# Retention of a chunk in three blocks between the seven products of an m-gate pair

## The chip, the core and the metric

The kernel runs as one program on one NeuronCore of a Trainium2 chip. The metric is the device time of one execution in microseconds (us). The kernel before was timed three times: 1814.88, 1816.7 and 1818.19 us, median 1816.7 us. A further execution was profiled; it took 1813.31 us, and its profile is the one read below.

## What is computed

The reference is one layer of a hybrid model on 1024 tokens of width 1024: a gated causal convolution and a retention (a linear attention with decay) whose outputs are gated and mixed, then a mixture of 32 experts, a per-layer embedding and a final norm. What the change touches is the retention and the sigmoid gates m_c and m_r:

```python
u, c_g, b_g, q, k, v, sg, m_c, m_r = jnp.split(h @ w_in[i], splits, axis=-1)
...
def step(state, inp):                 # a chunk of 128 tokens, 8 heads
    qb, kb, vb = inp
    scores = jnp.einsum('bhid,bhjd->bhij', qb, kb) * decay_mask
    inner = jnp.einsum('bhij,bhjv->bhiv', scores, vb)
    cross = jnp.einsum('bhid,bhdv->bhiv', qb, state) * q_decay[None, :, :, None]
    state = state * chunk_decay[None, :, None, None] + jnp.einsum(
        'bhjd,bhjv->bhdv', kb * k_decay[None, :, :, None], vb)
    return state, inner + cross
...
o = rmsnorm(o, g_ret[i].reshape(RET_HEADS, RET_DV)).reshape(b_, s_len, V_W)
y_ret = (jax.nn.silu(sg) * o) @ w_out_ret[i]
mixed = jax.nn.sigmoid(m_c) * y_conv + jax.nn.sigmoid(m_r) * y_ret
```

## The kernel before

The program is one long stretch for five engines. TensorE (PE) multiplies, VectorE (DVE) and ScalarE (ACT) move results out of PSUM and prepare operands, GpSimd (POOL) takes powers, and SyncE (SP) issues the DMAs. A scheduler turns the Python code into one fixed list of instructions for each engine; each engine then works through its list in order and waits at an instruction until its operands are ready. So where the scheduler puts an instruction decides what stands behind it when it waits.

Full-precision products are made from three passes: each operand is split into a rounded part and a remainder (`split`, L187: ACT writes the rounded part at L188, DVE the remainder at L189), and `mm3` (L192) multiplies high by high (L193), high by low (L194) and low by high (L195). All these matmuls have 512 columns.

The columns of `w_in` other than q, k and v are multiplied two blocks of 128 columns at a time, a *pair*, by `seven` (L390), which makes the four quarter products of a pair from seven products of half size instead of eight. Each of the seven is 12 matmuls (4 steps of k by 3 passes), into one of four PSUM accumulators called sa, sb, sc and sd. In the order of the code they are S2 into sb, S1 into sd, A11 into sa, S3 into sc, A12 into sa, S4 into sd and A22 into sc. Between A11 and S4 the sums u2 and u3 are formed (L417 on ACT; L418, L421 and L422 on DVE): L421 must have read sc before A22 writes into it, and L422 must have read sd before S4 does. The pieces of the weight (`pc`, six buffers for seven pieces of a pair) are prepared a pair ahead: L408 to L410 form three differences from the raw weight, which a DMA (L391) brings into one buffer, `both[:, 0]`.

The retention runs beside the eight m-gate pairs (L781 to L784): for pair n, `retention(n, ...)` puts chunk n into the program, then `gate_pair` the pair, then `turn()` the transposes that bring the chunk's output into columns. A chunk consists of eight transposes of q and k (L304, `qkp`), the scores (L314, `sp`; eight matmuls, which the trace shows as 16), the outputs (L325 and L329, `op`, in two halves of four heads), the product for the state (L359, `kv`) and the eight transposes of the output (L346, `otp`). In between DVE scales and masks (L306, L316), takes sums of squares (L337), normalises (L339) and updates the state (L364, L365), and ACT copies (L308, L333, L335, L349). No order between the chunk's matmuls and the pair's is written in the code; the scheduler mixes them.

After the m-gate pairs come twelve pairs for the convolution (`conv_pair`), four for `sg` (`sg_pair`), the mixing and output projections, the router, the experts and the end. They have no part in the change.

## Time and profile before

| | |
|---|---|
| three timed runs | 1814.88, 1816.7, 1818.19 us (median 1816.7) |
| the profiled execution | 1813.31 us, span 1811.5 us |
| PE busy | 1734.7 us, 96% of the span |
| DVE / ACT / POOL busy | 1267.3 / 901.3 / 161.2 us (70 / 50 / 9%) |
| chain that ended last | PE 42%, issue 4%, DMA 1%, DVE 1% |
| the m-gate pairs, first product to first conv product | 208.07 to 447.68 us |

The span is the time from the first to the last instruction in the profile. Busy times are those of the hardware profiler; PE's instructions overlap, so that a matmul of 0.39 us may start 0.23 us after the one before, and the useful number is the distance between two starts. "Idle before" is the time in which an engine had nothing running before an instruction, and the name behind the arrow is what the instruction waited for. The page's own costliest groups are the experts' weight splits and matmuls; the stage of the change is about 240 us of the span, and is read from the timeline.

### The profile page before, as it was taken

How to read it: one execution, taken by the hardware profiler on the slowest of the kernel's cores; microseconds unless marked ns; L12 is line 12 of the kernel's file. 1: busy time of each engine (PE TensorE's matmuls, PEld its weight loads, DVE VectorE, ACT ScalarE, POOL GpSimd, SP SyncE). 2: the span in 40 equal slices, each digit the busy share in tenths (PEclk: the TensorE clock that was granted, in tenths of full speed). 3: DMA queues.
4: the chain of work that ended last, by engine and by line, in shares of the span. 5: the costliest groups of instructions: out<-in, count | busy, mean ns of one | idle time of the engine just before them, and what ended most of it. 6: DMA issues, size and time to landing. Idle time of an engine off the chain costs nothing. (4 is left out here: it accounts for less than half of the span.)

```text
span 1811.5 us, 22815 instructions
## 1 busy us (share of the span) xinstructions
PE 1734.7 (96%) x8447; PEld 1347.0 (74%) x8447; DVE 1267.3 (70%) x1747; ACT 901.3 (50%) x1354; POOL 161.2 (9%) x157
## 2 busy tenths in 40 slices
PE   6999999999999999999999998999999999999697
PEld 5878777777778788778988986666666666666486
DVE  5559565655667776656454457999999988888674
ACT  4243343334222223434322336888888877777542
POOL 1000000000000000000000003212122221100010
PEclk9999999999999999999999989999999999999899
DMA  6534433333122216476665969999999999997561
GB/s 227 157 103 136 146 128 115 122 119 109 55 93 94 70 47 200 153 232 206 193 183 162 300 194 358 361 360 379 382 366 379 365 377 353 364 400 282 198 247 67
DMA packets 174629, 397.68 MB, mean 220 GB/s; under 512 B 14796, under 2 KB 101908, under 8 KB 148916
## 3 DMA queue, kind: packets, MB, share of 16 engines
q1 hardware_dynamic: 165012, 378.19, 60.2%
q0 software_dynamic: 9504, 18.02, 3.2%
q8 instruction: 67, 1.10, 0.3%
q14 instruction: 46, 0.38, 0.1%
HBM read 344.77 MB, written 57.68 MB: 222 GB/s over the span
## 5 line engine op out<-in xcount | busy, mean ns | idle before, releaser
L872 DVE TENSOR_TENSOR hc<-raw,hc 128x1024 fp32r<-128x1024 f32 x128 | 154.3, 1223 | 20.7 <-ACT hc L870 18.8
L872 DVE TENSOR_TENSOR hb<-raw,hb 128x1024 fp32r<-128x1024 f32 x128 | 153.8, 1219 | 15.2 <-ACT hb L870 14.3
L872 DVE TENSOR_TENSOR ha<-raw,ha 128x1024 fp32r<-128x1024 f32 x128 | 154.0, 1221 | 13.7 <-ACT ha L870 11.7
L870 ACT ACTIVATE ha<-raw 128x1024 fp32r<-128x1024 f32 x128 | 132.8, 1059 | 26.7 <-PE y L195 15.3
L870 ACT ACTIVATE hb<-raw 128x1024 fp32r<-128x1024 f32 x128 | 132.8, 1057 | 21.2 <-PE u L195 11.9
L870 ACT ACTIVATE hc<-raw 128x1024 fp32r<-128x1024 f32 x128 | 132.6, 1057 | 15.8 <-PE y L195 4.8
L188 ACT ACTIVATE pc<-both 128x512 fp32r<-128x512 f32 x120 | 73.0, 626 | 94.2 <-PE sd L195 31.1
L189 DVE TENSOR_TENSOR pc<-both,pc 128x512 fp32r<-128x512 f32 x120 | 81.2, 687 | 51.3 <-ACT pc L188 50.9
L188 ACT ACTIVATE pc<-bt 128x512 fp32r<-128x512 f32 x48 | 30.0, 625 | 153.0 <-DVE bt L410 137.2
L193 PE MATMUL y<-ph,wys 128*128 128x512 f32 x256 | 100.7, 394 | 4.9 <-ACT wys L188 4.9
L195 PE MATMUL y<-ph,wys 128*128 128x512 f32 x256 | 100.6, 393 | 1.2 <-DVE wys L189 1.2
L194 PE MATMUL y<-pl,wys 128*128 128x512 f32 x256 | 100.2, 391 | 0.0
L193 PE MATMUL sd<-sh,pc 128*128 128x512 f32 x192 | 77.0, 401 | 8.2 <-DVE u L422 8.0
L188 ACT ACTIVATE wys<-wyr 128x1024 fp32r<-128x1024 f32 x32 | 34.0, 1061 | 99.0 <-PE y L195 71.1
L195 PE MATMUL sd<-sh,pc 128*128 128x512 f32 x192 | 76.2, 397 | 0.0
L194 PE MATMUL sd<-sl,pc 128*128 128x512 f32 x192 | 75.4, 392 | 0.0
L189 DVE TENSOR_TENSOR wqs<-wqr,wqs 128x1024 fp32r<-128x1024 f32 x32 | 39.2, 1224 | 49.5 <-ACT wqs L188 49.5
L188 ACT ACTIVATE wqs<-wqr 128x1024 fp32r<-128x1024 f32 x32 | 33.9, 1059 | 70.3 <-PE qa L195 62.4
L718 POOL DMA_INDIRECT xgb<-h2d,ii x32 | 35.5, 1110 | 301.6 <-DVE hd L908 198.3
L193 PEld LDWEIGHTS y<-ph,wys 128*128 128x128 f32 x256 | 48.4, 189 | 15.4 <-ACT wys L188 5.7
L195 PEld LDWEIGHTS y<-ph,wys 128*128 128x128 f32 x256 | 48.5, 189 | 12.2 <-DVE wys L189 2.2
L506 DVE TENSOR_TENSOR msg<-y,msg 128x512 f32<-128x512 f32 x32 | 22.0, 689 | 50.2 <-PE y L195 50.1
(393 smaller groups left out, 4974.8 us busy)
## 6 DMA issues: line engine op xcount, KB each, us to landing
raw<-in_w_exp_gate_dram SPq DMA_DIRECT2D x64, 1024.0 KB, 19.7
raw<-in_w_exp_up_dram SPq DMA_DIRECT2D x64, 1024.0 KB, 19.7
raw<-in_w_exp_down_dram SPq DMA_DIRECT2D x63, 1024.0 KB, 21.8
both<-in_w_in_dram SPq DMA_DIRECT2D x24, 1024.0 KB, 5.8
wqr<-in_w_in_dram SPq DMA_DIRECT2D x32, 512.0 KB, 3.8
qd<-r SPq DMA_DIRECT2D x32, 256.0 KB, 3.1
both<-qd SPq DMA_DIRECT2D x8, 1024.0 KB, 4.8
wyr<-in_w_out_conv_dram SPq DMA_DIRECT2D x16, 512.0 KB, 4.5
```

The source lines that it names most:

```text
L188: a = A.activation(hi, src, AF.Copy)
L189: V.tensor_tensor(lo, src, hi, op=OP.subtract)
L193: T.matmul(o, lh, rh, start=start, stop=False, skip_group_check=skip)
L194: T.matmul(o, lh, rl, start=False, stop=False, skip_group_check=skip)
L195: T.matmul(o, ll, rh, start=False, stop=stop, skip_group_check=skip)
L506: V.tensor_tensor(sg, y, sg, op=OP.mult)
L718: g = P.indirect_dma_start(out=xgs[e % 3], out_offset=None, in_=h2d, in_offset=bass.IndirectOffsetOnAxis(ap=ii[:, 0, e:e + 1], axis=0), bo ...
L870: A.activation(hl[:, 0, q:q + 1024], raw[:, q:q + 1024], AF.Copy)
L872: V.tensor_tensor(hl[:, 1, q:q + 1024], raw[:, q:q + 1024], hl[:, 0, q:q + 1024], op=OP.subtract)
```

## The change

The chunk's work is cut into four functions that `retention` returns, and `seven` calls them at fixed places: `turned` after S2 (the transposes of q and k, and the transposes of the output of the chunk *before*, which are now made by `turn(n - 1)`), `scores` after S1, `outputs` after A11 (both halves of the outputs, and the state product), and `close` (normalising and the update of the state, DVE alone) behind the sum that writes u3. `tc.issue_after(x)` makes the scheduler put what follows behind x on x's engine; it adds no wait. With it the seven products and the three blocks stand on PE in the order of the code. The output of chunk 7 is turned after the last pair by `turn(7)`. The PSUM banks of the blocks are shared out anew (two banks for the transposes of q and k, two for the scores and two for the outputs, where each had one). No operation is added or left out.

```diff
     def mm3(o, lh, ll, rh, rl, start, stop, skip=False):
         T.matmul(o, lh, rh, start=start, stop=False, skip_group_check=skip)
         T.matmul(o, lh, rl, start=False, stop=False, skip_group_check=skip)
-        T.matmul(o, ll, rh, start=False, stop=stop, skip_group_check=skip)
+        return T.matmul(o, ll, rh, start=False, stop=stop, skip_group_check=skip).ins
...
+    osb = [t.rearrange("p (a b) -> p a b", a=4) for t in osbs]
+
+    def bank(name, tag):
+        return ps.tile([128, 4, 128], F32, name=name, tag=tag, bufs=1)
+
+    def turn(n):
+        t0 = n * 128
+        for b in range(2):
+            pt = bank("otp", ("o", "kv")[b])
+            for j in range(4):
+                pe = T.transpose(pt[:, j], osb[b][:, j], ident).ins
+            ot = w2k("ot").rearrange("p (a b) -> p a b", a=4)
+            for j in range(4):
+                A.activation(ot[:, j], pt[:, j], AF.Copy, scale=gret[:, 4 * b + j:4 * b + j + 1])
+            Y.dma_start(out=od[b * 512:(b + 1) * 512, t0:t0 + 128].rearrange("(a p) t -> p a t", p=128), in_=ot)
+        return pe
+
+
     def retention(n, ck):
         first, last = n == 0, n == 7
         Y.dma_start(out=ck, in_=qd[n * 128:(n + 1) * 128])
         q, k, v = ck[:, 0:512], ck[:, 512:1024], ck[:, 1024:2048]
...
+        qt, kt = (w2k(n_).rearrange("p (a b) -> p a b", a=4) for n_ in ("qt", "kt"))
+        sm, rss, kvs = [], [], []
+
+        def turned(pe):
+            for src, dst_, tag in ((q, qt, "tr"), (k, kt, "S")):
+                pt = bank("qkp", tag)
+                for a_ in range(4):
+                    pe = T.transpose(pt[:, a_], src[:, a_ * 128:(a_ + 1) * 128], ident).ins
+                if src is q:
+                    V.tensor_tensor(dst_, pt, qdT, op=OP.mult)
+                else:
+                    A.activation(dst_, pt, AF.Copy)
+            if not first:
+                with tc.issue_after(pe):
+                    pe = turn(n - 1)
+            return pe
+
+        def scores(pe):
+            for par in range(2):
+                sp = bank("sp", ("tr", "S")[par])
+                r = slice(par * 64, par * 64 + 64)
+                with tc.issue_after(pe):
+                    for a_ in range(4):
+                        pe = T.matmul(sp[:, a_], kt[r, a_], qt[r, a_], start=True, stop=True).ins
+                sb = w2k("sb").rearrange("p (a b) -> p a b", a=4)
+                V.tensor_tensor(sb, sp, caus[:, None, :].to_broadcast([128, 4, 128]), op=OP.mult)
+                sm.append(sb)
+            return pe
+
+        def outputs(pe):
             for b in range(2):
+                op = bank("op", ("o", "tr")[b])
+                m_ = 0
+                with tc.issue_after(pe):
+                    for a_ in (2 * b, 2 * b + 1):
+                        for par in range(2):
+                            h = 2 * a_ + par
+                            pe = T.matmul(op[:, h - 4 * b], sm[par][:, a_], v[:, h * 128:(h + 1) * 128],
+                                          start=m_ == 0, stop=first, skip_group_check=True).ins
+                            m_ += 1
+                        if not first:
+                            pe = T.matmul(op[:, (a_ % 2) * 2:(a_ % 2) * 2 + 2], qt[:, a_],
+                                          state[:, a_].rearrange("p (u v) -> p u v", u=2), start=False, stop=True,
+                                          skip_group_check=True).ins
+                A.activation(osb[b], op, AF.Copy)
+                sq = w2k("osq").rearrange("p (a b) -> p a b", a=4)
+                A.activation(sq, op, AF.Square)
+                ss = wk.tile([128, 8], F32, name="oss", tag="sm", bufs=4)
+                V.tensor_reduce(ss[:, 0:4], sq, axis=AX.X, op=OP.add)
+                rss.append(rstd(ss[:, 0:4], DV, "ors"))
+            if last:
+                return pe
+            kvs.append(bank("kv", "kv"))
+            with tc.issue_after(pe):
+                for a_ in range(4):
+                    for par in range(2):
+                        h = 2 * a_ + par
+                        pe = T.matmul(kvs[0][par * 64:par * 64 + 64, a_], k[:, h * 64:h * 64 + 64],
+                                      v[:, h * 128:(h + 1) * 128], start=True, stop=True, skip_group_check=True).ins
+            return pe
+
+        def close():
+            for b in range(2):
+                V.tensor_tensor(osb[b], osb[b], rss[b][:, :, None].to_broadcast([128, 4, 128]), op=OP.mult)
+            for par in range(0 if last else 2):
+                r = slice(par * 64, par * 64 + 64)
+                sv = state[r, :, par * 128:par * 128 + 128]
+                V.tensor_tensor(sv, sv, kvs[0][r], op=OP.add)
+                V.tensor_tensor(sv, sv, Gd[r, :, None].to_broadcast([64, 4, 128]), op=OP.mult)
+
+        return [turned, scores, outputs, close]
...
-    def seven(c0, raw, left, take):
+    def seven(c0, raw, left, take, mid=None):
         Y.dma_start(out=raw.rearrange("p (k n) -> p k n", k=8),
                     in_=w_in[:, c0:c0 + 256].rearrange("(k p) n -> p k n", p=128))
         b = raw.rearrange("p (q k s n) -> p q k s n", q=2, k=4, s=2)
...
             split(src, pc[:, 0], pc[:, 1])
             return pc
 
+
+        pe = []
+
+        def behind():
+            return tc.issue_after(pe[-1]) if mid and pe else nullcontext()
+
         def prod(o, i, pc, first):
             h, l, k0 = left[i]
-            for k in range(4):
-                mm3(o, pc[:, 0, k], pc[:, 1, k], h[k0 + k], l[k0 + k], first and k == 0, k == 3, True)
+            with behind():
+                for k in range(4):
+                    end = mm3(o, pc[:, 0, k], pc[:, 1, k], h[k0 + k], l[k0 + k], first and k == 0, k == 3, True)
+            pe.append(end)
+
+        def step(i):
+            if mid:
+                with behind():
+                    pe.append(mid[i](pe[-1]))
 
         V.tensor_tensor(t3, b22, b12, op=OP.subtract)
         V.tensor_tensor(b12, b12, b11, op=OP.subtract)
         V.tensor_tensor(t2, b22, b12, op=OP.subtract)
         a, b_, c, d = (acc(n) for n in ("sa", "sb", "sc", "sd"))
         prod(b_, 'S2', piece(t2), True)
+        step(0)
         prod(d, 'S1', piece(b12), True)
+        step(1)
         prod(a, 'A11', piece(b11), True)
         u2, u3, c21 = w2k("u2"), w2k("u3"), w2k("c21")
         with tc.high_priority():
             A.activation(u2, a, AF.Copy)
             V.tensor_tensor(u2, b_, u2, op=OP.add)
+        step(2)
         prod(c, 'S3', piece(t3), True)
         with tc.high_priority():
             V.tensor_tensor(u3, c, u2, op=OP.add)
-            V.tensor_tensor(u3, d, u3, op=OP.add)
+            summed = V.tensor_tensor(u3, d, u3, op=OP.add).ins
+        if mid:
+            with tc.issue_after(summed):
+                mid[3]()
...
-    def gate_pair(m, j, raw, left):
+    def gate_pair(m, j, raw, left, mid):
...
-        seven(6144 + m * 1024 + j * 256, raw(), left, take)
+        seven(6144 + m * 1024 + j * 256, raw(), left, take, mid)
...
-        turn = retention(n, both[:, 1])
-        gate_pair(n // 4, n % 4, raw, left)
-        turn()
+        gate_pair(n // 4, n % 4, raw, left, retention(n, both[:, 1]))
+    turn(7)
```

How the instructions stand now is shown at three places of a middle pair (the pairs 1 to 6 read alike). The first is PE's list from S1 on. Here `sb`, `sd` are the accumulators of S2 and S1, `sh`, `sl` the operand's two parts, `qkp` and `otp` the transposes. Before:

```order
L193 MATMUL sd<-sh,pc 128x512
L194 MATMUL sd<-sl,pc 128x512
L304 MATMUL qkp<-cs,both 128x128 x4
L195 MATMUL sd<-sh,pc 128x512
L193 MATMUL sd<-sh,pc 128x512
L194 MATMUL sd<-sl,pc 128x512
L195 MATMUL sd<-sh,pc 128x512
L193 MATMUL sd<-sh,pc 128x512
L194 MATMUL sd<-sl,pc 128x512
L304 MATMUL qkp<-cs,both 128x128 x4
```

And now:

```order
L194 MATMUL sb<-sl,pc 128x512
L195 MATMUL sb<-sh,pc 128x512
L323 MATMUL qkp<-cs,both 128x128 x8
L304 MATMUL otp<-cs,xgb 128x128 x8
L193 MATMUL sd<-sh,pc 128x512
L194 MATMUL sd<-sl,pc 128x512
```

The transposes of q and k, and those of the output, which stood in four runs of four, stand in one run of sixteen between two whole products.

The second place is PE's list from the end of A12 into sa to the start of S4 into sd. Before:

```order
L194 MATMUL sa<-hb,pc 128x512
L195 MATMUL sa<-hb,pc 128x512
L193 MATMUL sc<-hb,pc 128x512
L194 MATMUL sc<-hb,pc 128x512
L195 MATMUL sc<-hb,pc 128x512
L193 MATMUL sc<-hb,pc 128x512
L193 MATMUL sd<-sh,pc 128x512
L194 MATMUL sd<-sl,pc 128x512
```

And now:

```order
L194 MATMUL sa<-hb,pc 128x512
L195 MATMUL sa<-hb,pc 128x512
L193 MATMUL sd<-sh,pc 128x512
L194 MATMUL sd<-sl,pc 128x512
L195 MATMUL sd<-sh,pc 128x512
```

Four matmuls of A22 into sc stood ahead of S4; now S4 follows A12 directly, and A22 comes after it.

The third place is DVE's list from the masking of the scores (`sb<-sp`) to the sum that S4 waits for (the second of the two into the newer `u`, from `sd`). `xgb` holds the outputs that are normalised, `shared` the state, `oss` and `ors` the sums of squares and their roots. Before:

```order
L316 TENSOR_TENSOR sb<-sp,xgb 128x512
L408 TENSOR_TENSOR bt<-both 128x512
L316 TENSOR_TENSOR sb<-sp,xgb 128x512
L409 TENSOR_TENSOR both<-both 128x4x128
L410 TENSOR_TENSOR bt<-both 128x512
...
L365 TENSOR_TENSOR shared<-shared,xgb 64x4x128
L421 TENSOR_TENSOR u_2146<-sc,u_2145 128x512
L339 TENSOR_TENSOR xgb<-xgb,ors 128x512
L422 TENSOR_TENSOR u_2146<-sd,u_2146 128x512
```

And now:

```order
L341 TENSOR_TENSOR sb<-sp,xgb 128x512 x2
L441 TENSOR_TENSOR bt<-both 128x512
L442 TENSOR_TENSOR both<-both 128x4x128
L443 TENSOR_TENSOR bt<-both 128x512
...
L457 TENSOR_TENSOR u_2101<-sc,u_2100 128x512
L189 TENSOR_TENSOR pc<-both,pc 128x512
L458 TENSOR_TENSOR u_2101<-sd,u_2101 128x512
L379 TENSOR_TENSOR xgb<-xgb,ors 128x512 x2
L383 TENSOR_TENSOR shared<-shared,kv 64x4x128 x2
```

Both masks now stand ahead of the first use of the next raw weight, and the normalising and the state's update stand behind both sums; between the sums stands the remainder of one weight piece.

## Rows read from the trace of the kernel before

**Rows 1.** Windows: us from A to B, busy time of each engine, granted clock, DMA.

```profile
208.07:237.24 29.17, 27.38 (x145) 20.96 (x145) 21.22 (x37) 12.47 (x22) 2.70 (x2) 1.00 0.27 92
237.24:267.65 30.41, 29.44 (x158) 22.68 (x156) 17.63 (x30) 11.66 (x26) 2.31 (x2) 1.00 0.36 122
...
389.73:418.97 29.24, 28.29 (x143) 21.82 (x141) 16.50 (x28) 10.47 (x24) 2.32 (x2) 1.00 0.38 126
418.97:447.68 28.71, 28.28 (x143) 21.91 (x142) 15.22 (x28) 11.69 (x25) 2.01 (x2) 1.00 0.30 92
```

**Rows 2.** Waits from 237.2 to 419 us: us in total, times, longest.

```profile
DVE bt L408 <- DMA both<-in_w_in_dram: 11.2, 6, 2.4
...
PE sc L193 <- DVE u L421: 3.3, 6, 0.6
PE sd L193 <- DVE u L422: 2.4, 6, 0.4
```

**Rows 3.** Timeline of PE, pair 4: start, duration, line, operation [idle before].

```profile
330.36 0.66 PE L346 MATMUL otp<-cs,xgb 128*128 128x128 f32 x4
330.77 0.48 PE L195 MATMUL sb<-sh,pc 128*128 128x512 f32 x1
331.09 0.40 PE L193 MATMUL sb<-sh,pc 128*128 128x512 f32 x1
...
335.67 1.15 PE L314 MATMUL sp<-qt,kt 64*128 64x128 f32 x8
336.75 0.50 PE L193 MATMUL sa<-ha,pc 128*128 128x512 f32 x1
...
341.25 0.49 PE L325 MATMUL op<-both,sb 128*128 128x128 f32 x2 [0.40 <-DVE sb L316]
...
344.29 0.71 PE L325 MATMUL op<-both,sb 128*128 128x128 f32 x4
...
345.96 0.58 PE L194 MATMUL sc<-sl,pc 128*128 128x512 f32 x1
346.38 0.39 PE L195 MATMUL sc<-sh,pc 128*128 128x512 f32 x1
...
350.65 0.39 PE L195 MATMUL sa<-hb,pc 128*128 128x512 f32 x1
351.56 0.50 PE L193 MATMUL sc<-hb,pc 128*128 128x512 f32 x1 [0.53 <-DVE u L421]
351.90 0.40 PE L194 MATMUL sc<-hb,pc 128*128 128x512 f32 x1
...
352.36 0.40 PE L193 MATMUL sc<-hb,pc 128*128 128x512 f32 x1
353.16 0.50 PE L193 MATMUL sd<-sh,pc 128*128 128x512 f32 x1 [0.40 <-DVE u L422]
```

**Rows 4.** Timeline of PE at the end of the kernel: a run of eight transposes.

```profile
1734.76 1.04 PE L1135 MATMUL fpt<-cs,yb 128*128 128x128 f32 x8
1735.55 0.48 PE L193 MATMUL fo<-fh,fth 128*128 128x512 f32 x1
```

**Rows 5.** Timeline of PE at the start of pair 0.

```profile
211.50 0.50 PE L195 MATMUL sb<-sh,pc 128*128 128x512 f32 x1 [0.90 <-DVE pc L189]
```

**Rows 6.** Timeline of PE in the first conv pair.

```profile
463.60 0.50 PE L193 MATMUL sd<-sh,pc 128*128 128x512 f32 x1 [1.05 <-DVE u L422]
```

**Rows 7.** Timeline of all engines: one weight piece split after a product's end.

```profile
445.13 0.63 ACT L188 ACTIVATE pc<-both 128x512 fp32r<-128x512 f32 x1 [2.22 <-PE sd L195]
...
445.80 0.69 DVE L189 TENSOR_TENSOR pc<-both,pc 128x512 fp32r<-128x512 f32 x1 [2.58 <-ACT pc L188]
```

**Rows 8.** Timeline of SP: the issue of the raw weight's load in pair 1.

```profile
242.29 0.37 SPq L391 DMA_DIRECT2D both<-in_w_in_dram  x1
```

**Rows 9.** View of the tile `both`: its 33 loads, from issue to landing.

```profile
DMA to landing us min/median/max: 4.7/5.7/8.2
```

**Rows 10.** Timeline of PE, earlier in the kernel: a long wait.

```profile
112.62 0.63 PE L239 MATMUL xtq<-cs,xi 128*128 128x128 f32 x4 [3.44 <-issue]
```

**Rows 11.** Windows, as Rows 1: the stretch that follows that wait.

```profile
114.00:117.40 3.40, 3.40 (x8) 2.40 (x9) 2.67 (x6) 1.62 (x3) 0.55 (x1) 0.50 0.56 144
```

## The prediction

> **What bounds the kernel now.** I read the windows first, then the waits, then PE's timeline. The windows of the m-gate pairs [rows 1] show PE busy 27 to 29 of 29 to 30 us, DVE some 18 to 21, ACT 10 to 12 and the DMA engines at a third; so PE sets the length of this stage, and a microsecond that PE saves here comes off the end. The pairs 1 to 6 run from 237.24 to 418.97 us, 181.7 us or 30.29 each. The waits [rows 2] name what stops PE in them: in each of the six it waits twice for DVE's sums (L421, L422). PE's timeline of one pair [rows 3] shows the same two holes, and something the waits do not list: every time PE goes from the pair's matmuls to a few of the chunk's and back, it loses a tenth or two. The starts of two matmuls of 512 columns are 0.23 us apart (351.90 to 352.36, two steps); behind a run of transposes the next step is 0.32 (330.77 to 331.09), behind outputs 0.42 (345.96 to 346.38).

> **The change, part by part.** No operation is added or removed, so the 84 matmuls of a pair and the chunk's own work stay (scores 1.08 us a half, 335.67 to 336.75; outputs 1.67 a half, 344.29 to 345.96); what can change is waits and passages between them.

> *The two holes before A22 and S4.* From 350.65 to 351.56 PE needs 0.91 where 0.23 is normal, from 352.36 to 353.16 0.80; the first step behind each is 0.34 instead of 0.23 (351.56 to 351.90) [rows 3]. That is 0.68 + 0.57 + 2 x 0.11 = 1.47 us a pair. They arise because A22 starts right behind A12's end and L421 is late in DVE's list, behind the normalising and the state's update. In the new list S4 comes first, A22 last, and DVE has only one weight remainder (L189) between the sums L457 and L458. Does S4 still wait? Counted from the end of S3: L457, L189, L458 are 3 x 0.69 = 2.07 us, and ACT's half of L189 (0.63) runs beside L457 [rows 7]; A12 gives 12 x 0.23 = 2.76 us of cover. Some 0.5 us remain after the hand-overs between engines. I take the 1.47 as gone. If that cover fails, S4 waits by what is missing, and with it the whole rest of PE's list; behind L189 on DVE stand only L458 and what the next pair needs.

> *The mask behind the load.* DVE's first use of the raw weight (L408) waits for its load, 11.2 us in six pairs [rows 2], and the second mask stood behind it; PE waits 0.40 for the mask at 341.25 [rows 3]. Both masks now stand ahead. I take 0.2 as the mean of the six pairs (half of this one).

> *The transposes.* Four runs of four cost 0.41 + 0.09 each (330.36 to 330.77, and the step behind) [rows 3], 2.0 us. A run of eight takes 0.79 [rows 4], so four more cost 0.38; sixteen take 0.79 + 2 x 0.38 + 0.09 = 1.64. Saved 0.36. No row shows sixteen in a run, nor two kinds in one; I take 0.36, between nothing and twice that; a loss would need PE to wait within the run, for banks whose last readers are a block or more back. They need the chunk's load, which can start when the block of outputs has read the chunk before, three products (8.3 us) and S2 (2.8) ahead, and takes 8.2 at most [rows 9]; and outputs that the pair before has normalised.

> *Scores, outputs, state.* Before, they stand in four runs, the state product in a fifth together with transposes; now in two. Two passages less, at 0.09 to 0.19, and their entries: 0.3, between 0 and 0.6.

> *What is moved on the other engines.* ACT's eight copies of the turned outputs come a block earlier than the scores' masks need ACT, beside S1. SP issues the raw weight's load ahead of the two writes of the output instead of behind them; the write's time costs nothing, since nothing reads it before `sg_pair`. The powers on POOL have S3 to run beside. `close` puts four state operations and two normalisings, 6 x 0.69 = 4.1 us of DVE at the duration of rows 7, behind L458, ahead of the pieces t3 and b21 of the next pair, which are needed a whole pair later.

> A middle pair gains 1.47 + 0.2 + 0.36 + 0.3 = 2.33 us, six of them 14.0. Pair 0: PE is idle 29.17 - 27.38 = 1.79 us there [rows 1], 0.90 of it at 211.50 [rows 5], where DVE updates the state before it makes the first remainders. That update now comes later; a wait of 0.3 for the first remainder stays. Half an output's transposes (0.5) leave this pair, and the outputs merge (0.3): 0.6 + 0.9 + 0.5 + 0.3 = 2.3. Pair 7: idle 0.43, and 0.36 + 0.3 from the merging; with `turn(7)` whole behind it, the half turn in the first conv pair goes. But that conv pair's S4 waits 1.05 us for a sum behind a load [rows 6], and what PE reaches earlier there it partly waits: I subtract 0.4. Together 0.7. The sum is 14.0 + 2.3 + 0.7 = 17.0 us. The profiled execution took 1813.3 us (span 1811.5), so it would take 1796.3. The median of the timed runs is 3.4 us above the profiled one, and from it the same sum gives 1799.7 us, which I round to 1800.

> [...]

> **The rivals.** (1) *S4 waits in place of A22.* In a fixed order nothing fills a wait. For it: DVE's remainder between the two sums hangs on ACT, and the cover is only 0.5 us. Against it: DVE has little else there. With the wait of the conv pair, 1.05 us, in seven pairs, the gain is 17.0 - 7.4 = 9.6: 1807. (2) *The passages are free elsewhere*: the merged runs save nothing and only the waits go. Then 6 x 1.67 + 1.5 = 11.5, less 0.4: 1806; if they save twice my value, 6 x 3.0 + 3 = 21: 1796. [...] (4) *The raw weight's load comes too late: slower than before.* A new pair is about 28.0 us, S3 ends three products (8.3) before its end, at 19.7. Between the landing and L457 DVE has eight operations, L441 to L443, L453, two remainders and two sums of squares, 5.5 us at 0.69. So from a landing at 14.2 + 0.5 = 14.7 us on S4 waits, and from 17.0 on the whole 2.33 us are lost. The load is issued about 5 us into the pair (242.29 - 237.24) [rows 8] and takes 5.7, at most 8.2 [rows 9]: it lands at 10.7 to 13.3. The two output writes, now right behind it, speak for longer; that they ran beside it before, too, speaks against it. It would need 12 us; at 13 it lands at 18.0 and costs 3.3 in each of seven pairs, 23.1 against the 17.0: 1823. (5) *No change*: some fixed thing behind the stage, as that load in the first conv pair, gives all back; nothing shows one so long: the wait there is 1.05. That the change doesn't do what it says is excluded by the order.

> **How the numbers follow.** Chances: forecast 0.72 (own range 1795 to 1805), rivals 1 and 2 together 0.16, rival 3 0.03, rival 5 0.05, rival 4 0.04. The bounds of the merging and of the mask give 1794 at the best; to hold 8 in 10 the range reaches to rivals 1 and 2 and a little beyond: 1794 to 1809. About 0.2% (3.6 us) can be told from no change: faster are the forecast and rivals 1 to 3, 0.91; same rival 5, 0.05; slower rival 4, 0.04.

> **What would show it.** In the changed profile: pairs of about 28 us between the first products; no PE wait for L457 or L458; a step of 1.55 us from the first of sixteen transposes to S1; no PE wait for the masks; the raw weight landing 10 to 13 us after the pair's start; granted clock 1.00. Wrong would be: PE idle ahead of S4 or of the blocks in every pair, pairs over 29 us, or the clock at 0.50 in the stage.

## The result, and the profile after

The changed kernel takes 1789.5 us (median of 4 runs, 1787.9 to 1791.6), the kernel before 1816.0 beside it (1814.9 to 1818.2): a ratio of 0.9856, 95% interval 0.9842 to 0.9869. Between the two profiled executions (1813.3 and 1788.2 us) lie 25.2 us. The forecast was 1800, its range 1794 to 1809, from a gain of 17.0. The time lies 4.5 us below the range: the forecast was right in sign and place, and too small in size.

The windows of pairs 0, 1, 6 and 7 after the change (us from A to B, then the busy time of PE, PEld, DVE, ACT and POOL, the granted clock, DMA):

```profile
208.26:233.89 25.63, 25.63 (x142) 20.79 (x142) 19.95 (x34) 11.26 (x19) 2.33 (x2) 1.00 0.31 104
233.89:261.40 27.51, 27.51 (x158) 22.99 (x156) 18.11 (x30) 11.91 (x25) 2.01 (x2) 1.00 0.42 134
371.45:398.96 27.51, 27.51 (x157) 22.99 (x156) 18.04 (x29) 11.91 (x25) 2.01 (x2) 1.00 0.41 134
398.96:426.02 27.06, 27.06 (x149) 22.96 (x148) 16.08 (x27) 12.43 (x26) 2.01 (x2) 1.00 0.32 97
```

Against [rows 1], PE is never idle from pair 1 on: busy time and length are the same number. Pairs 1 to 6 take 27.51 us each, in place of 30.29. The waits of that stretch (us in total, times, longest) hold no row of PE any more; [rows 2] had two. What DVE waits for is now PE and, less, the load:

```profile
DVE u L457 <- PE sc L195: 12.0, 6, 2.0
...
DVE bt L441 <- DMA both<-in_w_in_dram: 6.7, 6, 1.3
```

PE's timeline of pair 5 (start, duration, line, operation), the counterpart of [rows 3]:

```profile
346.66 1.03 PE L323 MATMUL qkp<-cs,both 128*128 128x128 f32 x8
347.53 1.04 PE L304 MATMUL otp<-cs,xgb 128*128 128x128 f32 x8
348.32 0.48 PE L193 MATMUL sd<-sh,pc 128*128 128x512 f32 x1
...
351.25 1.71 PE L339 MATMUL sp<-qt,kt 64*128 64x128 f32 x16
352.89 0.50 PE L193 MATMUL sa<-ha,pc 128*128 128x512 f32 x1
353.22 0.39 PE L194 MATMUL sa<-ha,pc 128*128 128x512 f32 x1
...
358.84 0.60 PE L357 MATMUL op<-shared,qt 128*128 128x256 f32 x2
359.37 1.09 PE L373 MATMUL kv<-both 128*64 128x128 f32 x16
360.39 0.50 PE L193 MATMUL sc<-sh,pc 128*128 128x512 f32 x1
...
366.01 0.39 PE L193 MATMUL sd<-sh,pc 128*128 128x512 f32 x1
```

The transposes take 1.66 us (346.66 to 348.32), forecast 1.55; with the longer step behind them (0.32 in place of 0.23) 1.75, forecast 1.64. The surprise is the scores: both halves in 1.64 us (351.25 to 352.89), where one alone took 1.08 in [rows 3]. And S4 at 366.01 has no wait; DVE's timeline of the same pair says by how much:

```profile
363.49 0.69 DVE L457 TENSOR_TENSOR u<-sc,u 128x512 f32<-128x512 f32 x1 [2.00 <-PE sc L195]
364.15 0.69 DVE L189 TENSOR_TENSOR pc<-both,pc 128x512 fp32r<-128x512 f32 x1
364.76 0.68 DVE L458 TENSOR_TENSOR u<-sd,u 128x512 f32<-128x512 f32 x1
365.37 1.28 DVE L379 TENSOR_TENSOR xgb<-xgb,ors 128x512 f32<-128x512 f32 x2
```

The second sum ends at 365.44, 0.57 us ahead of S4; the normalising follows at once. Where the 25.2 us come from, by starts of first products: pairs 1 to 6 give 16.7 (6 x 2.78), pair 0 3.5 (29.17 to 25.63), pair 7 1.65 (28.71 to 27.06), the first conv pair 0.64 (21.49 to 20.85). That is 22.5. The other 2.7 lie outside: 2.9 behind the first conv pair, less 0.2 by which the stage starts later (208.26 in place of 208.07). In that conv pair PE still waits ahead of S4, 0.4 us longer than in [rows 6], as forecast:

```profile
441.30 0.50 PE L193 MATMUL sd<-sh,pc 128*128 128x512 f32 x1 [1.42 <-DVE u L458]
```

### The profile page after: what moved, and what is told of

Its sections match the earlier page's. It is cut to its first block, busy times and chain, and to the rows that moved or that the text cites. A ratio compares the mean times of both kernels' runs of the same rounds, so it can differ in the third digit from the quotient of the medians.

```text
span 1786.4 us, 22831 instructions
## 1 busy us (share of the span) xinstructions
PE 1720.2 (96%) x8447; PEld 1348.9 (76%) x8447; DVE 1269.6 (71%) x1747; ACT 903.3 (51%) x1354; POOL 157.6 (9%) x157
## 5 line engine op out<-in xcount | busy, mean ns | idle before, releaser
L910 DVE TENSOR_TENSOR hb<-raw,hb 128x1024 fp32r<-128x1024 f32 x128 | 153.9, 1220 | 15.2 <-ACT hb L908 13.8
L189 DVE TENSOR_TENSOR pc<-both,pc 128x512 fp32r<-128x512 f32 x120 | 81.2, 688 | 16.5 <-ACT pc L188 16.2
L189 DVE TENSOR_TENSOR wqs<-wqr,wqs 128x1024 fp32r<-128x1024 f32 x32 | 39.2, 1225 | 49.4 <-ACT wqs L188 49.2
L452 ACT ACTIVATE u<-sa 128x512 f32<-128x512 f32 x24 | 14.4, 598 | 98.6 <-PE sa L195 59.0
L193 PEld LDWEIGHTS y<-ph,wys 128*128 128x128 f32 x256 | 48.7, 190 | 14.0 <-ACT wys L188 4.2
```

Source lines behind the costliest of these rows:

```text
L189: V.tensor_tensor(lo, src, hi, op=OP.subtract)
L193: T.matmul(o, lh, rh, start=start, stop=False, skip_group_check=skip)
L910: V.tensor_tensor(hl[:, 1, q:q + 1024], raw[:, q:q + 1024], hl[:, 0, q:q + 1024], op=OP.subtract)
```

## The experiments

The whole time of a run turned out to wander by some microseconds behind the stage, so each kernel is read twice: by its median, and by the length from the first product of pair 0 to that of the first conv pair in its profile, which repeated to 0.01 us in the changed kernel (217.76, 217.77) and to 0.9 in the kernel before (239.61, 240.49).

| kernel | median us | pairs 1 to 6, us each | stage us | rest to the end us |
|---|---|---|---|---|
| before, two profiles | 1813.2 to 1816.0 (beside the others) | 30.29, 30.41 | 239.6, 240.5 | 1363.8, 1363.0 |
| after, twice | 1789.5, 1789.9 | 27.51 | 217.8, 217.8 | 1360.4, 1360.9 |
| scores apart | 1799.6 | 28.19 | 222.5 | 1366.3 |
| scores by turns | 1787.0 | 26.95 | 213.3 | 1362.3 |
| close early | 1817.0 | 30.1 to 31.7 | 244.5 | 1365.4 |
| small runs | 1792.5 | 27.55 | 218.6 | 1364.1 |
| one bank | 1853.6 | 34.1 to 38.0 | 277.4 | 1366.5 |
| turn in own pair | 1790.0 | 27.55 | 218.0 | 1361.1 |
| before, late close | 1800.6 | 28.0 to 30.5 | 229.3 | 1363.3 |
| before, late close, two banks | 1802.6 | 28.5 to 29.4 | 224.1 | 1368.5 |
| after, places free | 1790.1 (one run) | 27.51 | 217.0 | 1361.9 |
| scores and state by turns | 1783.2 | 26.27 | 209.5 | 1360.0 |

**The changed kernel again.** No edit.

> The changed kernel once more, beside the others. Theory: the gain belongs to the kernel, so about 1789.5 us (1787.5 to 1792) and a ratio of 0.985 to the kernel before. What lies behind the retention stage (some 2.8 of the 25.2 us between the two profiles) is either the kernel's too, then the router and the experts come as much earlier here as in the first profile, or it wanders from run to run, then this profile shows another number there while the retention pairs stay at 27.51 us each.

1789.9 us, ratio 0.9868 (0.9852 to 0.9883); every m-gate pair is the same to 0.01 us. Behind the stage it wanders: the first product of the router (tile `lp`) comes 424.6 us after the first conv product in the first profile of this kernel and 426.6 in the second, against 426.5 and 426.2 in the two profiles of the kernel before.

**Score halves apart.** Is the short run of scores worth what the timeline says?

```
 scores, between the halves:
+    if par == 0 and not first:
+        with tc.issue_after(pe):
+            pe = turn(n - 1)        # no longer in block 1
```

> The eight transposes of the last chunk's outputs stand between the two halves of the scores instead of ahead of S1; nothing else differs. Theory (the two halves, which use two different halves of the rows, run partly beside each other once they stand next to each other: sixteen records in 1.64 us, against 2 x 1.08 apart): apart they cost 1.08 each again, 0.52 us more in each of the seven pairs that have such transposes, 3.7 us in all, about 1793. Rival (the halves cost 1.08 in the kernel before because of what stood round them, the mask's wait and the restarts of the products): the block then takes 1.64 + 0.87 us, and the time stays at 1789.5.

```profile
353.54 1.16 PE L336 MATMUL sp<-qt,kt 64*128 64x128 f32 x8
354.63 1.09 PE L304 MATMUL otp<-cs,xgb 128*128 128x128 f32 x8
355.65 1.16 PE L336 MATMUL sp<-qt,kt 64*128 64x128 f32 x8
356.74 0.50 PE L193 MATMUL sa<-ha,pc 128*128 128x512 f32 x1
```

PE's timeline of pair 5: each half costs 1.09 again, 2.18 in place of 1.64, and the transposes, now between two other shapes, 1.02 in place of 0.79. A pair takes 0.68 more, 4.8 in the stage. The theory holds; the rival (the wait and the restarts round a half made it 1.08) falls: nothing waits here. The median is 1799.6, not the 1793 expected: it rose by 9.7, but 5.4 of it lie in the rest column, where the instructions are the same in kind and number.

**Scores by turns.** Overlap of the halves, or a fixed cost of each run?

```
-for par in range(2):          # half by half
-    for a_ in range(4): T.matmul(sp[:, a_], kt[r, a_], qt[r, a_], ...)
+for a_ in range(4):
+    for par in range(2): T.matmul(sps[par][:, a_], kt[r, a_], qt[r, a_], ...)
```

> The eight score matmuls in alternation, one of the upper rows, one of the lower, as kv already has them by columns; masks, banks and places are the same. Theory (halves run beside each other where they stand next to each other): sixteen records take what kv's sixteen take, 1.02 us, in place of 1.64: 0.6 us in each of eight pairs, 4.9 us, about 1784.6. Rival (a run of scores carries about half a microsecond once, at its entry or exit, and the second half only saves that): 1.64 us as before, 1789.5; or, if each change between the row halves costs something, longer, 1790 to 1800.

```profile
349.98 1.16 PE L339 MATMUL sp<-qt,kt 64*128 64x128 f32 x16
351.07 0.50 PE L193 MATMUL sa<-ha,pc 128*128 128x512 f32 x1
```

Sixteen records in 1.09 us (349.98 to 351.07): exactly what eight take in the experiment above. The second half is free when it alternates with the first. So it is overlap, and not a fixed cost of half a microsecond per run. The single records of the trace show it directly: here the first records of the two halves start 7 ns apart, at 349.98, and so do the others, two by two, while in the changed kernel the second half starts at 351.80, 0.55 us behind the first (351.25), so that only its beginning runs beside the first half's end. Pairs 26.95, 0.56 less, and 4.5 in the stage (4.9 expected); 1787.0 us, ratio 0.9845 (0.9832 to 0.9858).

**Close early.** VectorE's order differs; TensorE's is the same (ScalarE swaps two neighbours in a pair).

```
-summed = V.tensor_tensor(u3, d, u3, op=OP.add).ins
-with tc.issue_after(summed):
-    mid[3]()
+closed = mid[3]()                       # ahead of both u3 sums
+with tc.issue_after(closed): ...        # the two sums
```

> Only VectorE's order differs: the normalisation and the state's update (six instructions, 4.0 us) stand ahead of the two u3 sums; TensorE's order is the same, word for word. Theory (half of the change is VectorE's order: a late close keeps the sums ahead of S4): the second sum, which ends 0.57 us before S4 starts, ends about 3.0 us after that instead, worked out from VectorE's durations of 0.6 to 0.7 us an instruction and the two waits of 1.0 us for GpSimd's power; seven pairs make about 20 us, 1810. Rival (TensorE's fixed places carry it, VectorE's order is worth nothing with them): 1789.5, at most 1791.

The waits of PE in the eight pairs; then PE's timeline round S4 of pair 3, and windows of the same place (us from A to B, length, PE busy, granted clock, DMA):

```profile
PE sd L193 <- DVE u L462: 19.5, 8, 3.6
```

```profile
320.60 0.39 PE L195 MATMUL sa<-hb,pc 128*128 128x512 f32 x1
323.19 0.72 PE L193 MATMUL sd<-sh,pc 128*128 128x512 f32 x1 [2.20 <-DVE u L462]
323.71 0.63 PE L194 MATMUL sd<-sl,pc 128*128 128x512 f32 x1
324.13 0.63 PE L195 MATMUL sd<-sh,pc 128*128 128x512 f32 x1
```

```profile
318.00:321.00 3.00, 2.99 (x14) 1.00 0.47 199
...
324.00:325.00 1.00, 1.00 (x4) 0.50 0.28 109
...
327.00:328.00 1.00, 1.00 (x6) 1.00 0.00 0
```

The whole gain is gone, 1817.0 us (ratio 1.0015, 1.0004 to 1.0026), with PE's order unchanged. The stage is 26.7 longer than after, 20 expected. The waits make 19.5; the step ahead of each lasts 0.39 where starts are else 0.23 apart, and the one behind 0.34, 2.2 in eight; and in three of the eight pairs (mean granted clock 0.95, 0.95 and 0.94) the clock falls to 0.50 behind the wait, where some eight steps are 0.2 us longer each (0.43 in place of 0.23), 1.6 a time, 4.7. Together 26.4.

**Small runs.** The same matmuls in 37 more passages.

```
-step(0): q, k, and both halves of the turned outputs      step(2): outputs, kv
+step(0): q;  S1 behind k=0, 1, 2: k, half, half;  step(2): first outputs;
+S3 behind k=0, 1: second outputs, kv
```

> The same small matmuls on the same banks, at fixed places, but in more and shorter runs: the four sets of four transposes stand ahead of S1 and between its steps, the outputs of the second half and kv between the steps of S3; five more passages from 512-column products to small matmuls and back in each of pairs 1 to 6, four in pair 7, three in pair 0 (37 in all). Theory (short runs cost TensorE itself, apart from waits): from the last runs a passage into transposes and out costs 0.0 to 0.1 us (eight transposes took 0.79 and the next step 0.31), one into outputs, kv or scores 0.2 to 0.3; so pairs of 28.0 to 28.4 us in place of 27.51, some 4 to 6 us in all, about 1794. Rival (a passage is free and all that the three blocks saved was waits and the scores): 27.5 and 1789.9.

```profile
319.26 0.39 PE L195 MATMUL sb<-sh,pc 128*128 128x512 f32 x1
319.49 0.60 PE L325 MATMUL qkp<-cs,both 128*128 128x128 f32 x4
319.84 0.48 PE L193 MATMUL sd<-sh,pc 128*128 128x512 f32 x1
320.16 0.40 PE L194 MATMUL sd<-sl,pc 128*128 128x512 f32 x1
...
329.10 0.60 PE L356 MATMUL op<-shared,qt 128*128 128x256 f32 x2
329.53 0.61 PE L352 MATMUL op<-both,sb 128*128 128x128 f32 x4
329.98 0.60 PE L356 MATMUL op<-shared,qt 128*128 128x256 f32 x2
330.22 0.58 PE L193 MATMUL sc<-sh,pc 128*128 128x512 f32 x1
330.64 0.39 PE L194 MATMUL sc<-sl,pc 128*128 128x512 f32 x1
```

PE's timeline of pair 4. Pairs of 27.55 us: five more passages cost 0.04. My theory falls, and with it a reading in the prediction. The step of 0.32 behind the transposes is no loss: four transposes and one product take 0.67 (319.49 to 320.16), half of the 0.87 that eight transposes took in the profile after, and 0.23. Nor is the 0.42 behind outputs: two matmuls of the state and a product take 0.66 (329.98 to 330.64), where two of the state alone take 0.43 (329.10 to 329.53). So "it loses a tenth or two" at each passage was a misreading: the product starts early behind the run (at 330.22, 0.24 us behind the first of two matmuls that take 0.43 alone) and its long step gives that back. In [rows 3] the four transposes and a product took 0.73 (330.36 to 331.09); what such a passage cost before lay at its entry (0.41 from the first transpose to the product, 0.35 here). I put it down to operands that had only just come, which no run shows.

**One bank.** The two halves of a block share a bank, as before.

```
-(q, "tr"), (k, "S");  otp ("o", "kv")[b];  sp ("tr", "S")[par];  op ("o", "tr")[b]
+(q, "tr"), (k, "tr"); otp "tr";            sp "S";               op "o"
```

> The two halves of each block share a bank, as in the kernel before (transposes, scores and outputs each in one), at the same places. Theory (the second bank is what lets a block stand unbroken): each second half waits until its bank is read: about 1.0 us for the scaled q, 0.85 for kt, 1.6 for the four output copies, 1.0 for the mask and 0.54 for the overlap of the scores, 1.35 for the copy and the squares: 6.3 us a pair, 3.9 in pair 0, some 48 us in all, about 1838, more if TensorE's clock falls after such waits. Rival (the order alone does it, the banks add nothing): 1790.

```profile
PE otp L304 <- ACT ot L307: 7.5, 6, 1.3
PE sp L339 <- DVE sb L341: 7.2, 6, 1.6
PE op L353 <- ACT osq L362: 7.0, 6, 1.2
PE qkp L323 <- DVE qt L325: 4.7, 6, 0.8
PE otp L304 <- ACT kt L327: 4.4, 6, 0.7
```

The waits of six pairs: 30.8 us, 5.1 a pair, at the five places expected, and pairs of 35.1 on the mean, 7.6 longer. The stage is 60 us longer, not 48. A part of the surplus is the clock: the mean granted clock of pairs 0, 1, 2 and 7 is 0.95, 0.95, 0.87 and 0.95, and pairs 1 and 2 take 35.3 and 38.0 us, where pairs 3 to 6, at 1.00, take 34.1 to 34.6. Unbroken blocks with one bank are far worse than what was there before (ratio 1.0211, 1.0190 to 1.0231).

**Turned in the own pair.**

```
+gate_pair(...); with tc.issue_after(pes[-1]): pes.append(turn(n))   # no longer in block 1
```

> Each chunk's outputs are turned right behind A22 of its own pair, not in block 1 of the next; the rest is the same. Theory (that they come a pair later is worth something only by ScalarE: its eight copies of 0.34 us now stand between the pair's sigmoids and the next pair's pieces, so S1 waits about 1.0 to 1.5 us for its piece): 7 to 10 us more, about 1798. Rival (the place is free, one more passage of 0.1 us): 1790 to 1791.

1790.0 us, pairs 27.55: the rival holds. ScalarE has room for the eight copies there (in one pair two in 0.62 us and six in 1.67, the next weight piece right behind), S1 does not wait (it has no row among PE's waits); that the outputs are turned a pair later is worth nothing.

**Before, with the late close alone.**

```
 kernel before, seven():   V.tensor_tensor(u3, d, u3, op=OP.add)
+                          with tc.issue_after(summed): close()   # normalise, state
```

> The kernel before with one edit: the normalisation and the state's update come behind the two u3 sums on VectorE; TensorE's order is left to the scheduler, which has more or less the same runs as before. Theory (the waits ahead of S4 and A22, 1.47 us in a middle pair, come from VectorE's order alone): they go, and nothing else: 8 to 11 us less than before, about 1805, ratio 0.995. Rival (late close needs TensorE's fixed places; the scheduler makes another order with other waits of the same size): 1815, ratio 0.999 to 1.002.

The waits of PE in its pairs 1 to 7:

```profile
PE op L325 <- DVE sb L316: 1.5, 2, 1.3
```

Both waits for the sums are gone, as expected; two waits for masks stay, 1.3 us in one of the pairs 1 to 6 and 0.2 in pair 7. 1800.6 us, ratio 0.9913 (0.9891 to 0.9934), somewhat more than forecast; in the stage 10.3 us, 1.27 a middle pair (29.02 on the mean). About half of the change (21.9 in the stage) is this one move on VectorE.

**Before, late close and two banks.** Are the banks the other half?

```
-pt = trp("qkp") ... name="sp", tag="S" ... name="op", tag="o" ... trp("otp")
+tags as in the changed kernel; retention still ahead of the products
```

> The kernel before with the late close and the changed kernel's two banks for each block, but with the retention written ahead of the products as before and TensorE's order left to the scheduler, which now draws the whole chunk together behind S2: transposes, S2, then scores, outputs and kv almost next to one another, with only five kv matmuls and two product steps between scores and most outputs. Theory (what the fixed blocks give beyond the late close is distance: masks, copies and scaled q are ready long before their block): the first outputs wait for both masks, 0.3 + 2 x 0.6 us less 0.13 of kv, some 1.4 us a pair, while the adjoining score halves and the missing entries give back 0.5 and more; pairs of 28.4 to 28.9 us, 1797 to 1801. Rival (banks and late close are all of it): pairs of 27.5 us, 1790.

The waits of PE in pairs 1 to 6:

```profile
PE kv L368 <- ACT ot L349: 1.5, 3, 0.5
PE op L325 <- DVE sb L316: 0.7, 3, 0.2
PE sd L193 <- DVE u L427: 0.5, 1, 0.5
```

Pairs of 28.7 on the mean (28.5 to 29.4), as expected, but not by the expected road: the masks were to cost 1.4 us a pair, and cost 0.7 in all six. The stage is 5.2 us shorter than with the late close alone (224.1 against 229.3), and most of that is the scores again. With two banks the scheduler puts both halves into one run in all eight pairs, as in the changed kernel; PE's timeline in pair 3:

```profile
297.67 1.71 PE L314 MATMUL sp<-qt,kt 64*128 64x128 f32 x16
```

At 0.54 a pair that makes 4.3 of the 5.2. But the chunk's matmuls now follow on each other's heels, PE waits for masks and output copies, and kv is cut into several runs. The median, 1802.6 against an expected 1797 to 1801, does not show the gain; the rest is the longest of all (1368.5).

**After, places free.** The edges that fix TensorE's order are left out.

```
-with tc.issue_after(pe):       # four times, and behind() between products and blocks
+with nullcontext():
```

> The changed kernel without the edges that fix its blocks on TensorE: two banks, the late close and the program order of the blocks stay, the scheduler is free. Theory (banks and the late close carry the gain; fixed places carry none by themselves, since with nothing to wait for the scheduler has no reason to leave the program order): pairs 1 to 6 take 27.5 us as with fixed places; only pair 0, where some of kv is drawn ahead, differs by up to 1 us. Rival (the fixed places are what keeps the runs unbroken): 28 to 29 us a pair.

Pairs 1 to 6 take 27.51 again. With two banks, a late close and the blocks written where they belong, the scheduler has no cause to move anything; only pair 0 differs, 24.85 against 25.63.

**Before again.** No edit.

> The kernel before once more, for its profile. Theory (of the 25.2 us between the first two profiles only what lies in the retention stage and in conv pair 0, 22.4, belongs to the change; the rest is drift of transfers behind it): the pairs come as in the first profile to within some tenths (30.3 a middle pair), and the stretch from the first conv pair to the end, 1363.8 us there against 1360.4 in the changed kernel's first profile and 1360.9 in its second, comes out another 1 to 3 us away from 1363.8. Rival (the change speeds up what follows by 2 to 3 us): 1363.8 again, to within 0.5.

The rest is 1363.0, 0.8 from the first profile: between the two expectations. See below.

**Scores and state by turns.** On top of the scores by turns; op by even and odd heads, one bank each.

```
-T.matmul(op[:, two heads], qt[:, a_], state[:, a_], ...)     # 128 rows, 256 columns, half of them zero
+T.matmul(ops[h % 2][:, h // 2], qt[r, h // 2], state[r, h // 2, own 128], ...)   # h = 0 ... 7, 64 rows
```

> On top of the scores by turns, the state's terms of the outputs also go by row halves: eight matmuls of 64 rows and 128 columns in alternation (even heads from the upper rows into one bank, odd heads from the lower rows into the other) in place of four of 128 rows and 256 columns on a state whose other half is zero. Theory (two row halves run beside each other when they alternate): the sixteen records take 1.09 us, as the scores' sixteen did, in place of eight records of 0.218, 1.74; with one change more 0.55 to 0.65 us less in each of seven pairs: pairs of 26.3 to 26.4 us after 26.95, about 4 us in all, 1783 (1780 to 1786). Rival (alternation helps only where nothing is added up in PSUM): sixteen records of 0.11, 1.77 us, and 26.95 or a little more, 1787.

```profile
350.77 1.95 PE L352 MATMUL op<-both,sb 128*128 128x128 f32 x16
352.65 1.16 PE L356 MATMUL op<-shared,qt 64*128 64x128 f32 x16
353.74 1.09 PE L374 MATMUL kv<-both 128*64 128x128 f32 x16
354.77 0.50 PE L193 MATMUL sc<-sh,pc 128*128 128x512 f32 x1
```

The state's sixteen records take 1.09 us too, added up in PSUM or not; the theory holds. Pairs of 26.27 us, 1783.2 us (1780.7 to 1785.2), ratio 0.9830 (0.9817 to 0.9843): faster than both kernels.

## Why the prediction was right, and where it was wrong

*The holes before A22 and S4*, 1.47 a pair: right in kind. The late close alone gives 1.27, without a wait for the sums; moving it ahead of the sums costs more than the whole gain. The cover at S4, "some 0.5 us", is 0.57.

*Scores*: the step that failed. The text kept "scores 1.08 us a half" as work that stays and priced the passages of scores, outputs and state together at "0.3, between 0 and 0.6". Set next to each other in two banks, the halves, which use the upper and the lower 64 rows, run partly beside each other: 1.64 for both, 0.54 less in each of eight pairs, 4.3 us. (Separating them by transposes cost 0.68 a pair, with the changes of shape; what a separation by products, as before, costs beyond 0.54 was not measured.) That is most of the 5.5 us by which the stage and the first conv pair (22.5) exceed the sum of 17.0. It could have been asked of the trace before: kv's matmuls alternate between two column halves, and its sixteen records take no longer (1.02 us, 297.14 to 298.16) than eight of the scores did:

```profile
297.14 1.09 PE L359 MATMUL kv<-both 128*64 128x128 f32 x16
298.16 0.50 PE L193 MATMUL sb<-sh,pc 128*128 128x512 f32 x1
```

That two halves can run beside each other shows in the sixteen records of the scores by turns (1.09 us). Round a run of scores the runs show some 0.3 us (1.09 against 8 x 0.11 for a run of eight, at the 0.87 that eight transposes take, and 0.33 in place of 0.23 for the step behind it); where these come from no run shows.

*Transposes*, 0.36: about right, for a wrong reason. By small runs the merging is worth nothing; what went is the 0.06 by which a run of four took longer before (0.73 against 0.67), in four runs an estimated 0.24.

*The mask*, 0.2: in six pairs of the kernel before PE waited once for a mask, 0.4 us, in its second profile once, 1.0. The one that stays with the late close alone makes 1.3 in six pairs, 0.22 a pair. Counted from the late close, 1.27 + 0.54 + 0.24 + 0.22 = 2.27 of 2.78 are accounted for, an estimate, since the shares come from different kernels. The other 0.51 are the outputs, the state and the changes of shape, not taken apart further; the forecast had 0.3 for them together with the scores.

*Pair 0*: 3.5 in place of 2.3; 0.54 of the difference are the score halves. The late close alone brings 2.45 there. *Pair 7 and the first conv pair*: 2.3 in place of 0.7, of which again 0.54 by the scores; the wait in the conv pair did grow by 0.4. The rest of both surpluses was not taken apart.

*A loose reading*: the text has DVE at "some 18 to 21" us of a pair; [rows 1] shows 15.2 to 21.2. Nothing hangs on it.

*The rivals.* S4 does not wait in the pairs (1). The passages are free (2), but what was put down to them came from entries and overlap. Rival 3 of the chances, at 0.03, is a fall of the granted clock in the blocks, as to 0.50 in [rows 11]; that sixteen transposes bring one about no run shows: in the first profile of the changed kernel the clock is 1.00 through sixteen transposes in a run, 1.66 us (346.66 to 348.32), behind them (348.32 to 349.30) and in the windows of all eight pairs. The loads take 5.8 us in the median, 8.2 at most, and PE waits for none (4).

*What stays open*: the 2.7 us outside the stage and the first conv pair. Two profiles of each kernel agree to 0.8 there (1363.8 and 1363.0; 1360.4 and 1360.9), but the other kernels, with the same instructions, take 1360.0 to 1368.5 without any order by what was changed. I cannot say how much of the 2.7 belongs to the change. It matters for the miss: from the 1816.7 that the forecast starts from, the 22.5 of the stage and the conv pair alone would give 1794.2, the edge of the range. The scores brought the time to that edge; the 4.0 by which the medians (26.5 apart) go beyond 22.5 is not explained by any run.

What each part is worth, by the length of the stage: 239.6 before; 229.3 with the late close; 224.1 with two banks as well; 217.0 with the blocks written between the products; 217.8 with the places fixed. So the fixed places by themselves carry nothing. Of the 5.2 that the two banks bring, 4.3 are the adjoining scores. Writing the blocks between the products brings 7 us; 2.7 of them are the waits that the two-bank kernel shows in its middle pairs (1.5, 0.7 and 0.5), and the distance between a block and what it reads, which would explain the rest, is argued and not shown. Without the second bank the same places cost 60.

## What to carry to other kernels

Before matmuls of half the rows are priced as work that stays, look whether their two halves alternate: then the second half costs nothing here (1.09 us for sixteen records as for eight). In every run that shows it the two row halves wrote to a bank each, and the column halves of kv to one bank; whether row halves need two banks was not tried. On an engine that works in order, put what nobody waits for behind what the bottleneck waits for; that was half of this gain (10.3 of 21.9 us in the stage), and turning it round lost all of it (26.7). A longer step behind a run of small matmuls (0.32 and 0.42 us here, in place of 0.23) is not yet a loss: measure from the run's first start to the second step behind it.
